# A hybrid attention and mixture-of-experts layer on one core: when plain sums leave PSUM, which slots the router's tiles take, and where a count is read

## The chip, the cores and the metric

The kernel runs on 1 core of a Trainium2 chip. The metric is the device time of one execution in microseconds, as the median of a few runs. One more execution was profiled; all rows below are from that one. Its engines are PE (TensorE: matmuls; PEld is its weight load), DVE (VectorE), ACT (ScalarE), POOL (GpSimd) and SP (SyncE, which here only issues transfers and loads registers). PE, DVE and ACT share PSUM, the small memory into which matmuls add their sums.

## The reference

One decoder layer on 1024 tokens of width 1024. Everything is float32.

```python
h = rms_norm(x, norm1_g) * (1 + scale1) + shift1
aq, ak, av, bq, bk, bv = split(h @ w_in)
x = x + gate1 * (concat(dilated_attention(aq, ak, av), diff_attention(bq, bk, bv)) @ w_out)
h2 = rms_norm(x, norm2_g) * (1 + scale2) + shift2
logits = h2 @ w_router + b_router                  # 32 experts
top_val, top_idx = top_k(logits, 4); gates = softmax(top_val)
# every token goes to its 4 experts:
gu = xe @ w_gate_up[e] + b_gate_up[e]              # 1024 -> 2048
g = minimum(gu[:, :1024], 7); u = clip(gu[:, 1024:], -7, 7)
y = ((u + 1) * g * sigmoid(1.702 * g)) @ w_down[e] + b_down[e]
out = x + gate2 * sum over the token's experts of gate * y
```

## The kernel before

**Stages.** The kernel first makes projections and attention (to about 585 us). Then the router stage (to about 745 us) does the output projection block by block (8 blocks of 128 tokens), the second norm, the logits, the top 4 and each token's place in its experts' lists. The rest is 32 experts, one after another, fully unrolled, and a loop for tokens that did not fit an expert's planned capacity.

**Order.** From the attention stage on, the instructions of PE, ACT, DVE and SP stand in the order in which the Python code issues them (`manual_schedule`). POOL's order is chosen by a scheduler, which may bring an instruction forward as far as its data and its tile allow.

**Router (class `Block`).** For block b, `logits` makes the top 4, `places` (two blocks later) counts positions and fills `pay` (token number and gate, 4 pairs per token), `counted` makes `sli` (4 list places per token), and `scattered` has POOL write the 4 columns of `pay` into the table `tab` in device memory at the places in `sli` (L982, 4 indirect transfers per block). The token number in `pay` comes from a POOL iota (L944). A tile that comes from pool `sm` has 3 buffers (`sm3`, bufs=3), so block b takes the memory of block b-3 and its first writer waits until the last reader of that memory is done. A tile that comes from pool `rt` lives to the end. Only the last block takes `pay` and `sli` from `rt`. The same POOL queue also computes the reciprocal roots for the norms (L111), which DVE finishes (L115 to L117); then DVE makes `pay`, `hot` and `tg`, and PE multiplies these in `listed` (L960).

**An expert (function `expert`).** C is the expert's planned number of tokens (96 to 200; over 128 it is two blocks). Weights arrive in chunks of 1 MB, 12 per expert: 10 "split" chunks go through ACT (`hb`, high part, L826) and DVE (`ha`, low part, L813) into two halves each, through a ring of 6 chunk buffers; 2 "plain" chunks of `w_down` are used by PE as they are. `products` multiplies the split ones (L1196, L1202). After gate and up products come the plain chunks: `pg` is one PSUM tile with two banks; 4 sums (`place(0)` to `place(3)`), two per bank, over two halves `kh` of the inner dimension (L1252, 4 matmuls per sum and half in the code, two instructions each). In the second half ACT moves the sums out to `yl` with scale and bias (L1263): after `j == 1` sums 0 and 1, after `j == 3` sums 2 and 3. Then `between(kh)` transposes the next expert's tokens (L1174, and on ACT, DVE and POOL `xx`, `xb`), and `products(C, s_a, t0 + 16)` makes the other half of the output columns; `back` transposes (L1285), scales (`y`, L1286) and has POOL add the rows into the output (L1182). `banks()` takes one of 4 PSUM tiles in rotation. `done()` is a point at which transfers of later chunks are issued and later chunks are split, to targets fixed in a table: one half chunk is split at the `done()` after `j == 1` of the second half, one at the end of the half.

**Overflow.** `overflow()` (third expert) computes `tot`, the number of extra blocks. `nc.values_load(tot...)` (L1371) puts it into a register of each of the five engines, and `tc.For_i(0, n_over, 1)` (L1372) runs that many times.

Of the kernel before, what the change touches and what calls it, by code (L numbers as in the profile page):

```python
# [9 lines left out]
F32 = mybir.dt.float32  # L10
# [66 lines left out]
def hybrid_layer(ctx: ExitStack, tc: tile.TileContext, x, c_t, w_ada, b_ada_t, b_ada, norm1_t, w_in,  # L77
# [107 lines left out]
    with ExitStack() as st:  # L185
# [332 lines left out]
        with ExitStack() as so:  # L518
# [334 lines left out]
            class Block:  # L853
# [84 lines left out]
                def places(self):  # L938
                    pp = ps3.tile([P, 512], F32, name="po")
                    nc.tensor.matmul(pp[:, :E], upper, self.msk, start=True, stop=False)  # L940
                    nc.tensor.matmul(pp[:, :E], ones, mcum, start=False, stop=True)
                    nc.vector.reciprocal(self.den, self.den)
                    pay = (sm if self.b < NB - 1 else rt).tile([P, TOPK, 2], F32, name="pay")
                    nc.gpsimd.iota(pay.bitcast(I32)[:, :, 0], pattern=[[0, TOPK]], base=self.b * P, channel_multiplier=1)  # L944
                    nc.vector.tensor_scalar_mul(pay[:, :, 1], self.ge, self.den)

                    hot = sm.tile([P, len(BLOCKS0) * P], F32, name="hot", bufs=2)
                    nc.vector.tensor_scalar(hot, srow, pp[:, 0:1], self.msk[:, 0:1], op0=OP.is_equal, op1=OP.mult)
                    tg = sm.tile([P, 3], F32, name="tg")
                    nc.gpsimd.iota(tg[:, 0:1], pattern=[[0, 1]], base=self.b * P - S, channel_multiplier=1,  # L950
                                   allow_small_or_imprecise_dtypes=True)
                    nc.gpsimd.memset(tg[:, 2:3], 1.0)
                    g0 = sm.tile([P, TOPK], F32, name="g0")
                    nc.vector.tensor_mul(g0, self.sel[:, :, 0], pay[:, :, 1])
                    nc.vector.tensor_reduce(tg[:, 1:2], g0, axis=AX.X, op=OP.add)
                    self.hot, self.tg, self.pay, self.pp = hot, tg, pay, pp
# [13 lines left out]
                def counted(self):  # L970
                    pos = sm.tile([P, E], F32, name="pos")
                    nc.vector.tensor_add(pos, self.pp[:, :E], ebase)
                    nc.vector.tensor_mul(self.sel, self.sel, pos[:, None, :].to_broadcast([P, TOPK, E]))
                    slf = sm.tile([P, TOPK], F32, name="slf")
                    nc.vector.tensor_reduce(slf, self.sel, axis=AX.X, op=OP.add)
                    self.sli = (sm if self.b < NB - 1 else rt).tile([P, TOPK], I32, name="sli")
                    nc.vector.tensor_copy(self.sli, slf)
                    nc.vector.tensor_add(mcum, mcum, self.msk)

# [112 lines left out]
    with ExitStack() as se:  # L1092
# [30 lines left out]
        def done(high=0, low=0):  # L1123

            spent[0] += high
            spent[1] += low
            i, q = divmod(event[0], len(TG))
            event[0] += 1
            pump(i * NSP + TG[q])
            for t in todo:  # L1130
                t[0] -= 1
            while todo and todo[0][0] <= 0:
                todo.pop(0)[1]()
# [72 lines left out]
        def expert(i, st, between):  # L1206
            C, bc = st["C"], st["bc"]
            a = ap_.tile([P, KT, C], F32, name="ay")
            s_a = operand(C, "ax", "ab")
            t0, d0 = i * NSP, i * NCH + PLAIN[0]  # L1210

            def joined(dst, p, f, more):

                t = ap_.tile([P, 2, C], F32, name="tb", bufs=2)
                for j in range(2):
                    nc.scalar.activation(t[:, j], p[:, j, C:2 * C], AF.Identity, bias=bc[:, f + j:f + j + 1], scale=1.0)  # L1216
                if more:
                    nc.vector.scalar_tensor_tensor(dst, t, more, p[:, :, :C], op0=OP.add, op1=OP.add)
                else:
                    nc.vector.tensor_add(dst, p[:, :, :C], t)  # L1220

            for half in range(2):
                pg = products(C, st["x"], t0 + 8 * half)
                gt = ap_.tile([P, 4, C], F32, name="gt")
                for q in range(2):
                    joined(gt[:, 2 * q:2 * q + 2], pg[q], 4 * half + 2 * q, 0.0)
                sg = ap_.tile([P, 4, C], F32, name="su")
                nc.scalar.activation(sg, gt, AF.Sigmoid, scale=1.702)
                nc.vector.tensor_mul(gt, gt, sg)
                done(high=2, low=4)  # L1230
                pg = products(C, st["x"], t0 + 8 * half + 4)
                ut_ = ap_.tile([P, 4, C], F32, name="su")
                for q in range(2):
                    ut = ut_[:, 2 * q:2 * q + 2]
                    f = 4 * half + 2 * q
                    joined(ut, pg[q], KT + f, 1.0)
                    nc.vector.tensor_scalar(ut, ut, 8.0, -6.0, op0=OP.min, op1=OP.max)
                    nc.vector.scalar_tensor_tensor(a[:, f:f + 2], gt[:, 2 * q:2 * q + 2], GATE7, ut, op0=OP.min, op1=OP.mult)
                done(high=2, low=4)


            pg = banks()

            def place(j):
                return pg[:, j // 2, j % 2 * 256:j % 2 * 256 + C]

            ah, ab, _ = s_a
            for kh in range(2):
                raw = raws.pop(d0 + kh)
                for j in range(4):  # L1250
                    for k in range(4):
                        nc.tensor.matmul(place(j), raw[:, k, j * P:(j + 1) * P], a[:, 4 * kh + k],  # L1252
                                         start=(kh + k + j % 2 == 0), stop=(kh == 1 and k == 3 and j % 2 == 1))
                    if j == 1:
                        f = slice(4 * kh, 4 * kh + 4)
                        nc.scalar.activation(ah[:, f, :C], a[:, f], AF.Copy)  # L1256
                        nc.vector.tensor_sub(ah[:, f, C:], a[:, f], ah[:, f, :C].bitcast(F32))
                        nc.gpsimd.tensor_copy(ab[:, f], ah[:, f, :C].bitcast(F32))  # L1258
                    if kh and j % 2:
                        if j == 1:  # L1260
                            yl = ap_.tile([P, 4, C], F32, name="yl")
                        for f in (j - 1, j):
                            nc.scalar.activation(yl[:, f], place(f), AF.Identity,  # L1263
                                                 bias=bc[:, 2 * KT + f:2 * KT + f + 1], scale=g2c[:, f:f + 1])
                    if j == 1:
                        done()
                freed["p"] += 1
                done()
                between(kh)
            pg = products(C, s_a, t0 + 16)  # L1270
            yh = ap_.tile([P, KT, C], F32, name="ay")
            ys = [yl[:, f] for f in range(4)] + [yh[:, f] for f in range(4)]
            for j in range(4):
                f, p = 4 + j, pg[j // 2][:, j % 2]
                t = ap_.tile([P, 2, C], F32, name="tb", bufs=2)[:, 0]
                nc.scalar.activation(t, p[:, C:2 * C], AF.Identity, bias=bc[:, 2 * KT + f:2 * KT + f + 1], scale=g2c[:, f:f + 1])  # L1276
                nc.vector.scalar_tensor_tensor(ys[f], p[:, :C], g2c[:, f:f + 1], t, op0=OP.mult, op1=OP.add)  # L1277
            done(high=2, low=4)

            def back():  # L1280
                for (r0, n), sl in zip(st["blocks"], st["slots"]):
                    y = ap_.tile([P, D], F32, name="y", bufs=2)
                    py = banks().rearrange("p g (k c) -> p (g k) c", k=4)
                    for k in range(KT):
                        nc.tensor.transpose(py[:n, k], ys[k][:, r0:r0 + n], ident)  # L1285
                    nc.scalar.activation(y[:n].rearrange("p (k c) -> p k c", k=KT), py[:n], AF.Copy, scale=sl[:n, 1:2])  # L1286
                    scatter(y, sl, n)
            later(1, back)
# [66 lines left out]
        for i in range(E):  # L1355
            if i == 2:
                tot = overflow()
            nxt = stage_g(i + 1) if i + 1 < E else None
            expert(i, st, lambda g: nxt and stage_t(nxt, g))
            st = nxt  # L1360
# [4 lines left out]
    with ExitStack() as sf:  # L1365
# [2 lines left out]
        ps5 = sf.enter_context(tc.tile_pool(name="ps5", bufs=2, space=PSUM))  # L1368
        gate2 = fp.tile([P, D], F32, name="gate2")
        nc.sync.dma_start(gate2, bcast_rows(modd, 3 * D, D))  # L1370
        n_over = nc.values_load(tot[0:1, 0:1], min_val=0, max_val=P)  # L1371
        with tc.For_i(0, n_over, 1) as i:  # L1372
            ov = fp.tile([1, 2], I32, name="ov")
            nc.sync.dma_start(ov, ovd[ds(i, 1), :])
# [96 lines left out]
```

## Time and profile before

| | |
|---|---|
| median of 3 runs | 2157.39 us (2155.97 to 2163.31) |
| the profiled execution, device time | 2155.82 us |
| its span in the trace | 2154.0 us |
| mean granted PE clock over the span | 0.985 |
| PE matmul busy, share of the span | 95% |
| weight traffic and all else, mean | 255 GB/s over the span |

The span is the part of the device time that the trace covers; 1.8 us lie around it. A row's busy time of PE counts matmuls that overlap each other. An idle time in a row is put down to the event that ended it.

### The profile page before, as it was taken

Reading aid. Unit: us, or ns where it says so; the run is one execution under the profiler, and the core shown is the slowest. Engines: PE = TensorE matmul, PEld = TensorE weight load, DVE = VectorE, ACT = ScalarE, POOL = GpSimd, SP = SyncE. Lnnn points to the kernel's source line nnn. Section 1 sums busy time; section 2 is a strip of 40 time slices with the busy share of each in tenths; the row PEclk is TensorE's granted clock in tenths of the full one; section 3 lists DMA queues with packets and bytes.
Section 4 is the critical chain, followed back from the end, with each engine's and each line's share of the span. In section 5 each row is a group of like instructions: output and inputs, shape, how many; then the busy total and the mean of one; then the engine's idle time right before and its main releaser. Section 6 shows DMA issues by size and latency. Waiting matters only on the chain.

```text
span 2154.0 us, 43837 instructions
## 1 busy us (share of the span) xinstructions
PE 2046.7 (95%) x16922; PEld 1914.8 (89%) x16922; DVE 1631.7 (76%) x2838; ACT 1357.8 (63%) x2391; POOL 481.7 (22%) x466
## 2 busy tenths in 40 slices
PE   6999999999999699999999999999999999999997
PEld 6877778998887599999998999999999999999996
DVE  6587765776666778788787877878878878878884
ACT  3522314777643367677677677777877777768774
POOL 2245532111013411112111222112111211211211
PEclk9999999999999799999999999999999999999998
DMA  8267886442233498899799999989999999999993
GB/s 296 67 161 220 217 237 164 112 114 70 90 129 145 158 338 293 268 337 343 268 295 347 289 315 317 324 296 349 309 321 300 355 319 330 325 332 322 332 321 81
DMA packets 273655, 549.53 MB, mean 255 GB/s; under 512 B 31796, under 2 KB 31812, under 8 KB 273316
## 3 DMA queue, kind: packets, MB, share of 16 engines
q1 hardware_dynamic: 251507, 490.61, 67.4%
q0 software_dynamic: 21936, 56.09, 11.2%
q8 instruction: 134, 2.20, 0.4%
q14 instruction: 78, 0.63, 0.1%
HBM read 501.84 MB, written 44.78 MB: 254 GB/s over the span
## 4 chain that ended last, share of the span: by engine, by line
PE 61%; ACT 5%; DMA 3%; DVE 3%; issue 2%; POOL 1%; POOLq 0%; SPq 0%; ACTq 0%; DVEq 0%
PE gu L1196 30%; PE gu L1202 13%; PE gu L1252 10%; PE gu L1285 2%; ACT hb L826 2%; PE gu L1174 2%; PE po L605 1%; ACT yl L1263 1%; DMA eraw<-in_w_down_dram 1%; DMA eraw<-in_w_gate_up_dram 1%; PE pss L567 1%; DMA tab<-pay,sli 1%; PE pt L598 1%; POOL tab L982 1%; DVE ha L813 0%
## 5 line engine op out<-in xcount | busy, mean ns | idle before, releaser
L813 DVE TENSOR_TENSOR ha<-eraw,hb 128x1024 bf16<-128x1024 f32 x640 | 760.0, 1240 | 7.7 <-ACT hb L826 7.7
L826 ACT ACTIVATE hb<-eraw 128x1024 fp32r<-128x1024 f32 x640 | 634.1, 1050 | 21.2 <-DMA eraw<-in_w_down_dram 15.3
L1196 PE MATMUL gu<-xx,hb 128*128 128x256 f32 (+13 forms) x4096 | 586.3, 299 | 2.2 <-DVE xx L1178 2.2
L1196 PEld LDWEIGHTS gu<-xx,hb 128*128 128x128 f32 x4096 | 552.9, 189 | 2.6 <-DVE xx L1178 2.4
L1202 PEld LDWEIGHTS <-ha 128*128 128x128 bf16 x5120 | 310.6, 97 | 11.8 <-issue 1.5
L1252 PE MATMUL gu<-ay,draw 128*128 128x128 f32 (+19 forms) x2048 | 277.9, 292 | 36.4 <-ACT yl L1263 32.9
L1252 PEld LDWEIGHTS gu<-ay,draw 128*128 128x128 f32 x2048 | 260.5, 192 | 44.5 <-ACT yl L1263 39.7
L1202 PE MATMUL gu<-xb,ha 128*128 128x128 bf16 (+19 forms) x4096 | 271.6, 224 | 0.0
L1216 ACT ACTIVATE tb<-gu,bcol 128x128 f32<-128x128 f32 (+19 forms) x512 | 156.9, 369 | 89.8 <-PE gu L1202 80.8
L1182 POOL DMA_INDIRECT out_dram<-y,slot x47 | 79.7, 1695 | 404.9 <-ACT y L1286 263.0
L1146 POOL DMA_INDIRECT xg<-h2d,slot x47 | 65.9, 1401 | 393.0 <-PE gu L1174 86.8
L1196 PE MATMUL gu<-ax,hb 128*128 128x256 f32 (+13 forms) x1024 | 144.5, 298 | 0.0
L1276 ACT ACTIVATE tb<-gu,bcol,g2c 128x128 f32<-128x128 f32 (+19 forms) x128 | 56.3, 465 | 132.4 <-PE gu L1202 104.8
L1196 PEld LDWEIGHTS gu<-ax,hb 128*128 128x128 f32 x1024 | 137.4, 188 | 0.6
L571 DVE CUSTOM_DVE_ANT_0 p<-pss,bias 128x1024 f32<-128x1024 f32 (+7 forms) x128 | 94.4, 755 | 52.1 <-ACT p L580 23.5
L1277 DVE SCALAR_TENSOR_TENSOR ay<-gu,g2c,tb 128x128 f32<-128x128 f32 (+19 forms) x128 | 46.2, 362 | 113.9 <-ACT tb L1276 113.9
L1258 POOL CAST ab<-ax 128x512 bf16<-128x512 f32 (+19 forms) x64 | 69.7, 1094 | 263.7 <-ACT ax L1256 263.7
L605 PE MATMUL po<-vsb,pT 128*128 128x64 f32 (+1 forms) x864 | 111.3, 275 | 2.9 <-ACT pT L599 1.4
L605 PEld LDWEIGHTS po<-vsb,pT 128*128 128x128 f32 x864 | 105.4, 194 | 5.8 <-ACT pT L599 2.0
L580 ACT ACTIVATE p<-p,mn 128x1024 f32<-128x1024 f32 (+7 forms) x128 | 98.6, 773 | 11.9 <-DVE mn L571 11.2
L111 POOL TENSOR_TENSOR rrs<-vrs,nhalf 128x8 f32<-128x8 f32 (+2 forms) x48 | 66.1, 1377 | 169.6 <-DVE vrs L109 167.8
L459 PE MATMUL pp<-wh,hb 128*128 128x512 f32 x240 | 100.5, 419 | 0.0
(275 smaller groups left out, 3080.6 us busy)
## 6 DMA issues: line engine op xcount, KB each, us to landing
eraw<-in_w_gate_up_dram SPq DMA_DIRECT2D x256, 1024.0 KB
draw<-in_w_down_dram SPq DMA_DIRECT2D x64, 1024.0 KB
eraw<-in_w_down_dram SPq DMA_DIRECT2D x64, 1024.0 KB
wraw<-in_w_ada_dram SPq DMA_DIRECT2D x32, 512.0 KB
wraw<-in_w_in_dram SPq DMA_DIRECT2D x23, 512.0 KB
hb<-in_w_ada_dram SPq DMA_DIRECT2D x16, 512.0 KB
qd<-tt POOLq DMA_DIRECT2D x32, 256.0 KB, 3.7
kd<-tt POOLq DMA_DIRECT2D x32, 256.0 KB, 4.0
```

Source lines behind the costliest of these rows:

```text
L459: nc.tensor.matmul(pp, hh[b][:, k], wh[:, kk], start=(k == 0), stop=False)
L571: nc.vector.tensor_tensor_reduce(p[:, :n], pss[:, :n], bias[:, (NB - 1 - ib) * P:(NB - 1 - ib) * P + n], -1.0, 3.0e38, OP.add, OP.min, mn)
L580: nc.scalar.activation(p, p, AF.Exp, bias=self.mn[c], scale=-1.0, accum_out=self.l[:, c:c + 1])
L605: nc.tensor.matmul(self.po[:, :w], self.pT[:, k], vsb[self.br][:, k, self.h * w:(self.h + 1) * w], start=(k == 0), stop=(k == self.ib))
L813: nc.vector.tensor_tensor(parts[t][1], raws[c][:, 2 * q:2 * q + 2], parts[t][0].bitcast(F32), OP.subtract)
L826: nc.scalar.activation(h_, raws[c][:, 2 * q:2 * q + 2], AF.Copy)
L1182: nc.gpsimd.indirect_dma_start(out=out, out_offset=bass.IndirectOffsetOnAxis(ap=sl.bitcast(I32)[:n, 0:1], axis=0), in_=y[:n], in_offset=No ...
L1196: nc.tensor.matmul(pg[j // 2][:, j % 2, :max(256, 2 * C)], w[k][0][:, j * P:(j + 1) * P], xk[k], start=(k == 0), stop=False)
L1202: nc.tensor.matmul(pg[j // 2][:, j % 2, C:2 * C], w[k][1][:, j * P:(j + 1) * P], xb[:, k], start=False, stop=(k == KT - 1))
L1216: nc.scalar.activation(t[:, j], p[:, j, C:2 * C], AF.Identity, bias=bc[:, f + j:f + j + 1], scale=1.0)
L1252: nc.tensor.matmul(place(j), raw[:, k, j * P:(j + 1) * P], a[:, 4 * kh + k], start=(kh + k + j % 2 == 0), stop=(kh == 1 and k == 3 and j % ...
L1258: nc.gpsimd.tensor_copy(ab[:, f], ah[:, f, :C].bitcast(F32))
```

## The change

Three edits. In the router, `pay` and `sli` come from `rt` with one buffer per block, for every block. In the expert, the four sums of the plain half go to `yl` together, after `j == 3` of the second half, where before two of them went after `j == 1`; the `done()` after `j == 1` stays where it was, and so now stands ahead of all four. The register loads of `tot` move from ahead of the overflow loop to the start of the sixth expert (`i == 5`).

```diff
--- before.py
+++ after.py
@@ -940,7 +940,7 @@
                     nc.tensor.matmul(pp[:, :E], upper, self.msk, start=True, stop=False)
                     nc.tensor.matmul(pp[:, :E], ones, mcum, start=False, stop=True)
                     nc.vector.reciprocal(self.den, self.den)
-                    pay = (sm if self.b < NB - 1 else rt).tile([P, TOPK, 2], F32, name="pay")
+                    pay = rt.tile([P, TOPK, 2], F32, name="pay", bufs=NB)
                     nc.gpsimd.iota(pay.bitcast(I32)[:, :, 0], pattern=[[0, TOPK]], base=self.b * P, channel_multiplier=1)
                     nc.vector.tensor_scalar_mul(pay[:, :, 1], self.ge, self.den)
 
@@ -973,7 +973,7 @@
                     nc.vector.tensor_mul(self.sel, self.sel, pos[:, None, :].to_broadcast([P, TOPK, E]))
                     slf = sm.tile([P, TOPK], F32, name="slf")
                     nc.vector.tensor_reduce(slf, self.sel, axis=AX.X, op=OP.add)
-                    self.sli = (sm if self.b < NB - 1 else rt).tile([P, TOPK], I32, name="sli")
+                    self.sli = rt.tile([P, TOPK], I32, name="sli", bufs=NB)
                     nc.vector.tensor_copy(self.sli, slf)
                     nc.vector.tensor_add(mcum, mcum, self.msk)
 
@@ -1256,14 +1256,12 @@
                         nc.scalar.activation(ah[:, f, :C], a[:, f], AF.Copy)
                         nc.vector.tensor_sub(ah[:, f, C:], a[:, f], ah[:, f, :C].bitcast(F32))
                         nc.gpsimd.tensor_copy(ab[:, f], ah[:, f, :C].bitcast(F32))
-                    if kh and j % 2:
-                        if j == 1:
-                            yl = ap_.tile([P, 4, C], F32, name="yl")
-                        for f in (j - 1, j):
-                            nc.scalar.activation(yl[:, f], place(f), AF.Identity,
-                                                 bias=bc[:, 2 * KT + f:2 * KT + f + 1], scale=g2c[:, f:f + 1])
-                    if j == 1:
                         done()
+                if kh:
+                    yl = ap_.tile([P, 4, C], F32, name="yl")
+                    for f in range(4):
+                        nc.scalar.activation(yl[:, f], place(f), AF.Identity,
+                                             bias=bc[:, 2 * KT + f:2 * KT + f + 1], scale=g2c[:, f:f + 1])
                 freed["p"] += 1
                 done()
                 between(kh)
@@ -1355,6 +1353,8 @@
         for i in range(E):
             if i == 2:
                 tot = overflow()
+            if i == 5:
+                n_over = nc.values_load(tot[0:1, 0:1], min_val=0, max_val=P)
             nxt = stage_g(i + 1) if i + 1 < E else None
             expert(i, st, lambda g: nxt and stage_t(nxt, g))
             st = nxt
@@ -1368,7 +1368,6 @@
         ps5 = sf.enter_context(tc.tile_pool(name="ps5", bufs=2, space=PSUM))
         gate2 = fp.tile([P, D], F32, name="gate2")
         nc.sync.dma_start(gate2, bcast_rows(modd, 3 * D, D))
-        n_over = nc.values_load(tot[0:1, 0:1], min_val=0, max_val=P)
         with tc.For_i(0, n_over, 1) as i:
             ov = fp.tile([1, 2], I32, name="ov")
             nc.sync.dma_start(ov, ovd[ds(i, 1), :])
```

## Rows read from the trace of the kernel before

**Rows 1.** The page's first section: busy us (share of the span) and instructions.
```profile
PE 2046.7 (95%) x16922; PEld 1914.8 (89%) x16922; DVE 1631.7 (76%) x2838; ACT 1357.8 (63%) x2391; POOL 481.7 (22%) x466
```

**Rows 2.** Waits, 780 to 2154 us: waiter, releaser, total us, times, longest.
```profile
PE gu L1252 <- ACT yl L1263: 32.9, 32, 3.2
PE gu L1252 <- DVE ay L1238: 2.5, 2, 2.1
```

**Rows 3.** Timeline of one expert, 918 to 942 us: start, us, engine, line.
```profile
921.68 3.79 PE L1252 MATMUL gu<-ay,draw 128*128 128x128 f32 x32
...
925.31 0.94 PE L1174 MATMUL gu<-ident,xg 128*128 128x128 f32 x8
...
926.18 2.05 PE L1252 MATMUL gu<-ay,draw 128*128 128x128 f32 x16
...
928.27 0.81 ACT L1263 ACTIVATE yl<-gu,bcol,g2c 128x128 f32<-128x128 f32 x2 [0.33 <-PE gu L1252]
928.97 1.05 ACT L826 ACTIVATE hb<-eraw 128x1024 fp32r<-128x1024 f32 x1
929.13 2.05 PE L1252 MATMUL gu<-ay,draw 128*128 128x128 f32 x16 [0.90 <-ACT yl L1263]
...
931.01 0.94 PE L1174 MATMUL gu<-ident,xg 128*128 128x128 f32 x8
931.22 0.81 ACT L1263 ACTIVATE yl<-gu,bcol,g2c 128x128 f32<-128x128 f32 x2 [1.20 <-PE gu L1252]
...
931.88 4.06 PE L1196 MATMUL gu<-ax,hb 128*128 128x256 f32 x32
...
934.28 1.34 DVE L1178 TENSOR_TENSOR xx<-gu,xx 128x1024 fp32r<-128x1024 f32 x2
...
937.56 2.25 PE L1196 MATMUL gu<-xx,hb 128*128 128x272 f32 x16
```

**Rows 4.** Windows: stretch, us, busy PE, PEld, DVE, ACT, POOL, PEclk, DMA share, GB/s.
```profile
1339.00:2070.00 731.00, 714.57 (x7047) 700.13 (x7046) 603.72 (x801) 551.79 (x882) 141.71 (x128) 1.00 0.98 325
1468.00:1511.00 43.00, 42.08 (x409) 41.48 (x409) 35.79 (x48) 32.49 (x52) 7.93 (x8) 1.00 1.03 353
```

**Rows 5.** Waits of ACT's splits for weights, 780 to 2154 us; columns of Rows 2.
```profile
ACT hb L826 <- DMA eraw<-in_w_down_dram: 14.4, 9, 7.6
ACT hb L826 <- DMA eraw<-in_w_gate_up_dram: 5.8, 3, 2.9
```

**Rows 6.** Waits in the router, 629.7 to 702.6 us.
```profile
POOL pay L944 <- DMA tab<-pay,sli: 10.5, 4, 3.2
DVE qr L115 <- POOL rr L111: 6.2, 4, 2.1
...
PE p L960 <- DVE tg L955: 5.0, 4, 2.3
```

**Rows 7.** Windows of the router where the granted clock is low; columns of Rows 4.
```profile
661.00:664.00 3.00, 3.00 (x9) 2.31 (x9) 1.11 (x5) 1.76 (x5) 0.00 (x0) 0.50 0.43 175
694.90:701.70 6.80, 6.80 (x27) 6.11 (x27) 4.73 (x12) 2.48 (x7) 0.17 (x2) 0.50 0.19 77
```

**Rows 8.** Timeline of POOL, 0 to 30 us.
```profile
3.61 0.20 POOL L944 IOTA pay<- 128x4 int32 x1
21.14 1.01 POOL L111 TENSOR_TENSOR rrs<-vrs,nhalf 128x1 f32<-128x1 f32 x1 [17.33 <-DVE vrs L109]
```

**Rows 9.** Instructions of L1371: duration ns min/median/max, first and last start.
```profile
L1371 SPq TENSOR_LOAD <-tot x1: 757/757/757, 850.0 to 850.0; - x1
L1371 PEldq TENSOR_LOAD <-tot x1: 484/484/484, 2140.6 to 2140.6; - x1
...
L1371 POOLq TENSOR_LOAD <-tot x1: 502/502/502, 2142.1 to 2142.1; - x1
```

**Rows 10.** Timeline of the end, 2139 to 2144 us.
```profile
2142.38 1.46 POOL L1182 DMA_INDIRECT out_dram<-y,slot  x1 [12.81 <-ACTq L1372]
```

**Rows 11.** Waits of SP, 2128 to 2155 us.
```profile
SPq L1372 <- DMA out_dram<-y,slot: 4.5, 1, 4.5
```

## Prediction

> **What bounds the kernel now.** I read the page first, then the waits of PE, then a timeline of one expert. PE is busy 95% of the span [rows 1], so time is won only where PE waits, runs at a lower clock, or restarts. In the expert stage PE's waits have one cause that repeats: 32 times, once in each expert, it waits for ACT's `yl`, 32.9 us in all [rows 2]. The timeline shows where: the first half of the plain sums runs 32 matmul instructions without a stop, the second half runs 16, stands still while ACT moves the first two sums out, and runs 16 more [rows 3]. Next I read what feeds PE. The transfers are nearly full: between 1339 and 2070 us they move 325 GB/s at a busy share of 0.98, and the fullest stretch reaches 353 GB/s [rows 4]; ACT's splits already wait 20.2 us (14.4 + 5.8, 12 times) for weights that are late [rows 5]. Last come the waits of the router [rows 6] and the windows in which PE's granted clock is low there [rows 7].
>
> **Experts: the sums leave together.** With all four evacuations behind the last product nothing of L1263 stands between PE's matmuls. What that gives is read from one expert: the first half takes 925.31 - 921.68 = 3.63 us up to the next PE work, the second 931.01 - 926.18 = 4.83 us [rows 3]. The difference, 1.20 us, is the 0.90 us of waiting and the 0.3 us that PE loses when its matmuls run out and start again. 32 x 1.20 = 38.4 us. Of the 32.9 us of waiting, 32 x 0.90 = 28.8 us are regular; the other 4.1 us belong to a few experts in which ACT came late [rows 2]. Those go too, unless ACT's lateness meets PE elsewhere; between 0 and 4.1 I take 2 us.
>
> What it adds: ACT's evacuations end later. Four take about 2 x 0.81 = 1.62 us after the last sum instead of 0.81. Two things stand behind them. First, a PSUM tile: four rotate, and where the next expert has two blocks (16 of 32 experts) the transposes take two, so the second tile of the following products is the one that `yl` is read from. In the expert shown the last sum ends at 931.18, so the four would end at 932.84; PE starts those products at 931.88 and is at their second tile after 8 of 32 matmuls, 4.06 / 4 = 1.0 us later, at 932.9 [rows 3]. It just fits. From nothing to 0.12 us in 16 experts is 0 to 2 us; I take 1. Second, the next tokens' `xx`: DVE ends it at 935.62 and PE needs it at 937.56 [rows 3]; 0.81 of these 1.94 us are used up, so this costs nothing. Without that cover it would be up to 0.81 us per expert. The split of 1.05 us that now stands ahead of the four runs while PE multiplies, where ACT was waiting for PE before.
>
> The clock has no term here: in the long stretch of experts the granted clock is 1.00, waits and all [rows 4]. By the Trainium skill ("TensorE: Matmul & The Clock Gate", "A second HAM failure mode") short idle times between groups of matmuls can make the clock swing; by it 32 waits would each have a slow piece behind them, and if each were the 3.0 us at half speed of the router [rows 7], another 32 x 1.5 = 48 us would come back. The trace does not agree, and I leave it out.
>
> **What the faster experts ask of the transfers.** 38.4 us of a stage of 1374 us (780 to 2154) is 2.8%: 325 GB/s become 334, under the 353 that a full stretch moved [rows 4]. So it fits on average, not everywhere. A late chunk becomes later by what PE gained since the queue last had room. If that is one or two experts (1.2 to 2.4 us) at each of the 12 places, ACT waits 14 to 29 us more. So far PE pays a third of ACT's waits: the 4.1 us above and 2.5 us for `ay` [rows 2] of 20.2 us. A third of 14 to 29 is 5 to 10; the ends are 0 and 29. I take 6 us.
>
> **Router: own slots.** Four times POOL's iota for `pay` waits for the scatters into `tab` to land, 10.5 us in all. Behind it on POOL stand the roots of the norms (L111); DVE waits for those 6.2 us, and PE then waits 5.0 us for `tg` [rows 6]. With a slot per block no iota takes memory that a scatter still reads. Like the one that lies in `rt` now, the iotas can run at the start, where POOL has 17.33 us of idle time and 8 x 0.20 us find room [rows 8]; without that cover they cost 1.6 us. DVE's 6.2 us cover PE's 5.0 us, so the 5.0 goes, less perhaps 0.5. After two of these waits PE's granted clock is 0.50, its 1.2 GHz level, for 3.0 and 6.8 us [rows 7]; 9.8 us at half speed is 4.9 us lost. If the waits go the clock may stay up. From 0 to 4.9 I take 3.5. Together 8 us, between 3 and 10. The handover to the first expert stays as long and starts earlier.
>
> **The count's registers.** The load of 0.50 us on POOL at the end [rows 9] runs while POOL's last scatter starts (2142.1 and 2142.38 [rows 10]), and SP then waits 4.5 us for that scatter to land [rows 11]. So taking it away gives 0 to 0.5 us; I take 0. In the sixth expert PE's load takes 0.48 us [rows 9], between nothing (matmuls already handed out cover it) and 0.5; ACT, DVE and POOL behave alike, and SP (0.76 us) has waits of its own. I take 0.4.
>
> **Sum**, against the profiled execution's 2155.82 us: -38.4 - 2 + 1 + 6 - 8 + 0.4 = -41.0, so 2114.8, and 2115 us is my prediction. The median of the runs is 1.6 us above that execution, inside the range.
>
> **Rivals.**
> - Transfers are the bound. For: busy share 0.98 and 20.2 us of ACT waits [rows 4, 5]. Against: 353 GB/s in a full stretch. Then the 29 us all fall on PE in place of 6: 2138 us. Chance 0.17.
> - The router's wait moves. PE finds the next thing late (ACT or DVE), or the clock falls all the same; the router gives nothing: 2123 us. For: POOL, DVE and PE form one chain there. Against: DVE's saving is larger than PE's wait [rows 6]. Chance 0.10.
> - The wait stays. Sums 0 and 1 lie in another bank than the one PE writes next, so what holds PE may be no read of theirs. Then only the router counts: 2155.8 - 8 + 0.4 = 2148 us. Against: PE goes on 0.05 us after the second `yl` ends (929.08, 929.13 [rows 3]), and 32 of 32 waits name it [rows 2]. By the Trainium skill ("PSUM — Partial Sum Buffer", "Summary: rules for kernel authors") one reads PSUM during matmuls from a different bank and evacuates promptly; by that rule the early evacuation would cost nothing, and the change would only hold the tile longer. The trace disagrees with the first part. Chance 0.05.
> - Slower than before: ACT comes late to all four, because the split ahead of them waits for weights, and in the 16 experts with a two-block successor PE stops at the tile. It decides from 41 / 16 = 2.6 us each; at 3.2 us each, the longest wait so far [rows 2], 51 us go and it ends at 2166. Against: 12 late chunks in all [rows 5]. Chance 0.04.
>
> **Numbers.** The forecast itself (2105 to 2124) has 0.64. Its lower end takes all 4.1, 10 and no loss to transfers: 2155.8 - 38.4 - 4.1 - 10 = 2103. The range reaches up into the first two rivals: 2105 to 2130. About 0.3% (6.5 us) is what a measurement of this kernel can tell from no change. Faster by more than that: forecast, the first two rivals and about half of the third, 0.93; within: 0.03; slower: 0.04.
>
> **What would show it.** After: no wait of PE L1252 for `yl`; both halves of the plain sums 3.6 us long where C is 128; no wait of `pay` for `tab`, and eight iotas at the start; granted clock 1.00 in the router up to the handover; ACT's waits for weights at 30 to 50 us. It is wrong if a wait of about 1 us stands before the second tile of the following products, if ACT's waits for weights reach PE in most experts, or if L960 waits as before.

## The result, and the profile after

The kernel after takes 2110.61 us (median of 4 runs, 2109.98 to 2113.01), the kernel before, now with 4 runs, 2158.26 us. The ratio is 0.9778, 95% interval 0.9759 to 0.9797. The forecast was 2115 us, range 2105 to 2130. The profiled execution after takes 2109.98 us, 45.84 us less than the one before. I cut both traces at three points that each has (first gate matmul of the router, L878; first expert product, L1196; end of the last matmul) and compared the pieces:

| stretch, us | before | after | change | predicted |
|---|---|---|---|---|
| up to the router | 586.13 | 584.28 | -1.85 | 0 |
| router | 159.83 | 152.79 | -7.04 | -8 |
| 32 experts | 1394.99 | 1358.20 | -36.79 | -33.0 |
| tail | 13.09 | 12.93 | -0.16 | 0 |

The first line is spread between executions: nothing there was changed, and over the first six runs below this stretch differs from the one before by +0.3 to -2.2 us, whichever edits the kernel has.

The page's first section, after (answers to [rows 1]):

```profile
PE 2035.8 (97%) x16922; PEld 1910.2 (91%) x16922; DVE 1635.9 (78%) x2838; ACT 1355.8 (64%) x2391; POOL 493.8 (23%) x466
```

PE has as many instructions as before and is busy for a larger share of a shorter span. Waits of PE after, from the first expert's products on, 741 to 2108 us (answers to [rows 2]); the first two rows of the answer:

```profile
PE gu L1252 <- DVE ay L1238: 4.4, 4, 1.9
PE gu L1283 <- DVE ay L1275: 0.5, 1, 0.5
```

The row of 32.9 us for `yl` is gone; what stands at the top now was the second row before. Timeline of the same place in the same expert, 905 to 925 us (answers to [rows 3]):

```profile
909.27 3.79 PE L1252 MATMUL gu<-ay,draw 128*128 128x128 f32 x32
...
912.90 0.94 PE L1174 MATMUL gu<-ident,xg 128*128 128x128 f32 x8
...
913.77 3.84 PE L1252 MATMUL gu<-ay,draw 128*128 128x128 f32 x32
...
917.45 0.94 PE L1174 MATMUL gu<-ident,xg 128*128 128x128 f32 x8
917.65 1.51 ACT L1263 ACTIVATE yl<-gu,bcol,g2c 128x128 f32<-128x128 f32 x4 [1.15 <-PE gu L1252]
...
918.32 4.06 PE L1196 MATMUL gu<-ax,hb 128*128 128x256 f32 x32
...
921.90 1.34 DVE L1178 TENSOR_TENSOR xx<-gu,xx 128x1024 fp32r<-128x1024 f32 x2
...
923.99 1.25 PE L1196 MATMUL gu<-xx,hb 128*128 128x272 f32 x8
```

Both halves are now one row of 32 matmuls, 3.63 us (909.27 to 912.90) and 3.68 us (913.77 to 917.45) up to the next work of PE. The four evacuations end at 917.65 + 1.51 = 919.16; the following products begin at 918.32 and are at their second tile 1.0 us later, at 919.3, and their row is 4.06 us long, as before. DVE ends `xx` at 923.24, and PE takes it at 923.99: the cover has shrunk from 1.94 to 0.75 us, and it still holds.

A window of the expert stage (answers to [rows 4]; same columns):

```profile
1300.00:2030.00 730.00, 728.86 (x7196) 716.88 (x7195) 621.66 (x822) 563.52 (x904) 153.09 (x134) 1.00 0.99 335
```

ACT's waits for weights, 740 to 2108 us (answers to [rows 5]):

```profile
ACT hb L826 <- DMA eraw<-in_w_down_dram: 28.0, 14, 6.9
ACT hb L826 <- DMA eraw<-in_w_gate_up_dram: 6.7, 3, 3.4
```

The transfers give 335 GB/s, as worked out (334), and the splits wait 34.7 us; in the whole expert stage before, counted from 740 us as here, it was 21.1 us. PE is busy 728.86 of 730 us all the same.

The mean clock of 1.00 over such a window hides short pieces at the lower level. Before, one lies in the expert stage, just ahead of the window of [rows 4] and behind the longest of the 32 stops. PE's timeline there, and a window:

```profile
1326.50 3.72 PE L1252 MATMUL gu<-ay,draw 128*128 128x140 f32 x16 [3.17 <-ACT yl L1263]
```

```profile
1326.30:1329.70 3.40, 3.20 (x14) 3.20 (x15) 3.40 (x5) 1.09 (x2) 2.60 (x1) 0.50 1.04 392
```

After, there are two, in the second halves of the ninth and the thirteenth expert, each behind a stop for `ay`:

```profile
1126.37 5.90 PE L1252 MATMUL gu<-ay,draw 128*128 128x140 f32 x32 [1.90 <-DVE ay L1238]
...
1299.56 0.74 PE L1252 MATMUL gu<-ay,draw 128*128 128x140 f32 x4 [1.87 <-DVE ay L1238]
```

```profile
1126.50:1129.90 3.40, 3.40 (x14) 3.14 (x15) 3.33 (x6) 3.40 (x5) 0.20 (x1) 0.50 0.85 313
1300.50:1303.90 3.40, 3.15 (x13) 3.15 (x14) 3.40 (x5) 3.26 (x5) 0.00 (x0) 0.51 1.00 350
```

Each such piece of 3.4 us at half speed costs some 1.7 us: the 32 matmuls at 1126.37 take 5.90 us, and the 32 of the same expert's first half take 4.03.

In the router the eight iotas now stand together at the start. POOL's timeline, 0 to 30 us (answers to [rows 8]):

```profile
3.62 0.74 POOL L944 IOTA pay<- 128x4 int32 x8
21.30 1.01 POOL L111 TENSOR_TENSOR rrs<-vrs,nhalf 128x1 f32<-128x1 f32 x1 [16.94 <-DVE vrs L109]
```

POOL's waits in the router no longer name `tab` for `pay`, and this is PE's only wait in 629 to 703 us (answers to the last of [rows 6]):

```profile
PE p L960 <- DVE tg L955: 0.2, 1, 0.2
```

The clock did not stay up throughout. Windows of the router (answers to [rows 7]):

```profile
655.30:658.30 3.00, 3.00 (x11) 2.37 (x10) 1.13 (x4) 1.76 (x5) 0.00 (x0) 0.52 0.42 175
658.30:662.00 3.70, 3.70 (x17) 3.02 (x16) 3.39 (x14) 0.72 (x2) 1.04 (x1) 0.93 0.60 210
662.00:679.00 17.00, 17.00 (x95) 14.41 (x95) 11.23 (x37) 6.80 (x24) 6.66 (x9) 1.00 0.50 187
679.00:697.00 18.00, 17.95 (x102) 14.73 (x100) 11.83 (x37) 7.21 (x25) 7.42 (x10) 1.00 0.44 161
```

PE's timeline ahead of the first of them:

```profile
652.86 0.58 PE L960 MATMUL p<-tg,hot 128*128 128x3 f32 x4 [0.16 <-DVE tg L955]
653.29 1.95 PE L918 MATMUL po<-wr,hT 128*128 128x32 f32 x16
655.08 0.48 PE L878 MATMUL pm<-hb,oh 128*128 128x512 f32 x1
655.39 0.60 PE L879 MATMUL pm<-hb,ol 128*128 128x512 f32 x1
```

One low piece of some 3 us is left (0.52, close to the lower level of 1.2 GHz), where before there were two, of 3.0 and 6.8 us. Ahead of it PE waited 0.16 us only, and ran 20 matmuls of 3 and 32 columns. The same 20 run in the next two blocks at 1.00. In the trace of the run that evacuates after the third product (below) PE has the same wait here (0.15 us), and its clock is not low in the router before 714 us. So neither the wait nor the narrow matmuls alone tell when the clock falls.

Past 703 us there is a wait that the kernel before did not have. The place matmul of the seventh block, before and after:

```profile
717.01 0.30 PE L940 MATMUL po<-msk,upper 128*128 128x32 f32 x2
```

```profile
708.07 0.41 PE L940 MATMUL po<-msk,upper 128*128 128x32 f32 x2 [1.79 <-DVE nm L933]
```

Counted from the start of the router, PE comes here 8.9 us earlier than before, and then waits 1.79 us for DVE.

The loads of the count, two rows of the line's instructions (answers to [rows 9]):

```profile
L1357 PEldq TENSOR_LOAD <-tot x1: 485/485/485, 962.1 to 962.1; - x1
...
L1357 POOLq TENSOR_LOAD <-tot x1: 505/505/505, 2096.5 to 2096.5; - x1
```

The end in the timeline (answers to [rows 10]):

```profile
2096.70 1.46 POOL L1182 DMA_INDIRECT out_dram<-y,slot  x1 [11.72 <-ACTq L1371]
```

SP's wait there, 2085 to 2109 us (answers to [rows 11]):

```profile
SPq L1371 <- DMA out_dram<-y,slot: 4.3, 1, 4.3
```

PE's load moved to the sixth expert; POOL's, whose order the scheduler makes, stayed at the end.

### The profile page after: what moved, and what is told of

Its sections match the earlier page's. It is cut to its first block, busy times and chain, and to the rows that moved or that the text cites. A ratio compares the mean times of both kernels' runs of the same rounds, so it can differ in the third digit from the quotient of the medians.

```text
span 2108.2 us, 43814 instructions
## 1 busy us (share of the span) xinstructions
PE 2035.8 (97%) x16922; PEld 1910.2 (91%) x16922; DVE 1635.9 (78%) x2838; ACT 1355.8 (64%) x2391; POOL 493.8 (23%) x466
## 4 chain that ended last, share of the span: by engine, by line
PE 62%; DVE 4%; DMA 4%; ACT 2%; issue 2%; POOL 0%; POOLq 0%; SPq 0%; ACTq 0%; DVEq 0%
PE gu L1196 30%; PE gu L1202 13%; PE gu L1252 11%; DMA eraw<-in_w_down_dram 2%; PE gu L1283 2%; PE gu L1174 2%; PE po L605 1%; DMA eraw<-in_w_gate_up_dram 1%; DVE ha L813 1%; PE pss L567 1%; PE pt L598 1%; PE pm L880 0%; PE pm L878 0%; PE pm L879 0%; ACT hb L826 0%
## 5 line engine op out<-in xcount | busy, mean ns | idle before, releaser
L1196 PE MATMUL gu<-xx,hb 128*128 128x256 f32 (+13 forms) x4096 | 586.6, 299 | 2.5 <-DVE xx L1178 2.5
L1196 PEld LDWEIGHTS gu<-xx,hb 128*128 128x128 f32 x4096 | 553.3, 189 | 3.1 <-DVE xx L1178 2.8
L1252 PE MATMUL gu<-ay,draw 128*128 128x128 f32 (+19 forms) x2048 | 271.5, 291 | 4.4 <-DVE ay L1238 4.4
L1182 POOL DMA_INDIRECT out_dram<-y,slot x47 | 78.3, 1667 | 390.6 <-ACT y L1284 225.9
L1146 POOL DMA_INDIRECT xg<-h2d,slot x47 | 71.7, 1525 | 339.7 <-DVE ay L1238 89.6
L1196 PE MATMUL gu<-ax,hb 128*128 128x256 f32 (+13 forms) x1024 | 145.0, 299 | 0.2 <-DVE ax L1257 0.2
L1196 PEld LDWEIGHTS gu<-ax,hb 128*128 128x128 f32 x1024 | 137.5, 188 | 1.3 <-DVE ax L1257 0.5
L1220 DVE TENSOR_TENSOR gt<-gu,tb 128x256 f32<-128x256 f32 (+19 forms) x128 | 55.4, 445 | 60.8 <-ACT tb L1216 53.1
```

The lines of the kernel that those rows point to most:

```text
L1146: nc.gpsimd.indirect_dma_start(out=xg[:n], out_offset=None, in_=h2d, in_offset=bass.IndirectOffsetOnAxis(ap=sl.bitcast(I32)[:n, 0:1], axis=0))
L1182: nc.gpsimd.indirect_dma_start(out=out, out_offset=bass.IndirectOffsetOnAxis(ap=sl.bitcast(I32)[:n, 0:1], axis=0), in_=y[:n], in_offset=No ...
L1196: nc.tensor.matmul(pg[j // 2][:, j % 2, :max(256, 2 * C)], w[k][0][:, j * P:(j + 1) * P], xk[k], start=(k == 0), stop=False)
```

## The experiments

Theory: PE waited for `yl` because the evacuation reads the tile that the next product writes, though in another bank; without that wait the experts are worth some 37 us and the router's slots 7 us, and the late weights take little back. Theories of the wait, as the expectations name them: the order between evacuation and product is kept for a whole PSUM tile, or it has to do with the bank or with the moment. Other rivals: the transfers are now the bound; `sli`'s slots count too; the count's loads cost time. Three groups of kernels ran, each beside the kernel before on the same chip (2152.02, 2153.72 and 2155.27 us); the ratios are to that.

**One edit at a time.** Each kernel is the one before with one of the three parts of the diff.

The sums only:

> The kernel before with only the expert's edit: all four sums go to yl after the last one. My theory: this edit carries nearly all of the gain. The expert stage was 1395.0 us before and 1358.2 us with all edits, so it should be about 37 us shorter here, the two halves of the plain sums equally long, and the time 36 to 39 us below before; the router's waits for the landing of tab (10.5 us) stay. Rival, that the edits need each other (a router that ends earlier gives the transfers a lead on which the experts then draw): the expert stage gains clearly less than 37 us, 25 to 32.

2119.72 us, ratio 0.9844 (0.983 to 0.9858). Experts 1359.06 us, router 159.75, as before; PE still waits for `tg` there (3.8 us in 630 to 703 us).

The slots only:

> The kernel before with only the router's edit: pay and sli with a slot per block. My theory: 7 us less, all of it between the start of the router (586.1 us before) and the first product of the first expert (746.0), and an expert stage as long as before (1395). The 1.85 us that the kernel with all edits gained ahead of the router are chance: then they need not be here. Rival: POOL standing at the first pay until the attention stage frees its memory (37 us of waiting) cost those 1.85 us; then they are here too, and the total is 9 us.

2148.74 us, ratio 0.9975 (0.9963 to 0.9987). Router 152.55 us (-7.28), experts 1396.46 us; the waits for `yl` stay (31.8 us, 32 times). So each edit acts in its own stage. By their ratios the two kernels gain 33.6 and 5.3 us, less than the 36 to 39 and the 7 expected. The stages shorten by 35.9 and 7.3 us, but that is against the one trace of before, whose execution took 2155.82 us; before has a median of 2152.02 us in this group. So a difference of two stages can be off by a few us.

The count only:

> The kernel before with only the register loads of the count moved into the sixth expert. My theory: nothing that can be measured, from -0.5 to +0.5 us; the stretch from PE's last product to the end stays at 13.1 us. Rival: the loads at the end cost what they last, and 0.5 us or more go there; or PE stands for its 0.48 us in the sixth expert and the time rises by that.

2156.27 us, ratio 1.0015 (1.0004 to 1.0025). I had not expected a loss. At the sixth expert nothing is to be seen: measured from the first expert product, the plain sums start 0.4 us later than before in each of the first six experts alike, and 0.3 in the next two. Steps come later: -1.0 us at the ninth expert, +1.5 at the tenth, +1.8 at the fourteenth. The two traced executions differ by 0.4 us in all (2156.19 and 2155.82), so these traces do not hold the loss that the medians show.

**All edits, and all but the count.**

> The kernel with all three edits again, beside kernels with fewer. The single edits measured -33.6 us (sums), -5.3 us (slots) and +3.2 us (count): -35.7 us together, while all edits at once had measured -47.8 us (ratio 0.9778) beside another set of runs of before. My theory: the edits add up, and the difference is that of one set of runs to the next; then this one measures a ratio between 0.979 and 0.983 (36 to 45 us). Rival: the edits need each other; then the ratio is again 0.978 or lower.

> All edits but the count's: the register loads stand ahead of the overflow loop as before. My theory: the same as all edits within 2 us, since the register loads run beside other work at either place. Rival: the 3.2 us by which the count's edit alone came out slower are real; then this kernel is about 3 us faster than all edits.

2113.15 us, ratio 0.9807 (0.9793 to 0.982), and 2110.79 us, 0.9799 (0.9785 to 0.9812). The intervals overlap. The two part by 1.8 us at the thirteenth expert and are 1.0 us apart at the stage's end, so again nothing happens where the loads stand. The count's edit gives nothing; whether it costs 1 to 3 us, by shifting when weights land or otherwise, was not settled.

**Bank or tile: evacuating after the third product.** All edits, but sums 0 and 1, in the first bank of the tile, leave after product 2 and not after product 3:

```diff
-                if kh:
-                    yl = ap_.tile([P, 4, C], F32, name="yl")
-                    for f in range(4):
...
+                    if kh and j > 1:
+                        if j == 2:
+                            yl = ap_.tile([P, 4, C], F32, name="yl")
+                        for f in ((0, 1) if j == 2 else (2, 3)):
```

> The kernel with all edits, except that sums 0 and 1 go to yl after the third sum (j == 2) and sums 2 and 3 after the fourth. Sums 0 and 1 are in the tile's first bank, the third and fourth in its second. Theory A: what held PE is that any read of the tile by ACT is put in order with every later write to the tile, whichever bank. Then PE now stands ahead of the fourth sum, in every expert, for about 0.9 us (ACT reads the first two only when the third is done), and the time is back near before: 2140 to 2160. Theory B: only accesses to one bank are put in order. Then the fourth sum waits for nothing and the time is that of all edits, 2110. Theory C: PE was held at the first write to the second bank only, by something else than yl: no wait ahead of the fourth sum, 2110, and a wait ahead of the third as before would come back.

2147.92 us, ratio 0.9974 (0.9964 to 0.9985). The gain in the experts is gone. PE's waits, 741 to 2150 us, first row:

```profile
PE gu L1252 <- ACT yl L1264: 32.3, 32, 3.4
```

The same expert in its timeline:

```profile
917.13 2.94 PE L1252 MATMUL gu<-ay,draw 128*128 128x128 f32 x24
...
920.11 0.81 ACT L1264 ACTIVATE yl<-gu,bcol,g2c 128x128 f32<-128x128 f32 x2 [0.26 <-PE gu L1252]
...
920.97 1.16 PE L1252 MATMUL gu<-ay,draw 128*128 128x128 f32 x8 [0.90 <-ACT yl L1264]
```

Now 24 matmuls run, PE stands still for the same 0.90 us, and 8 follow. ACT reads one bank, product 3 goes to the other, which product 2 has already written; the only thing the two share is the tile. The trace names what holds PE: the weight load at 920.97 waits for a semaphore that ACT's second evacuation raises. Before, the first weight load of product 2 waits for it (929.12). The order is thus one that the program's instructions keep.

**The reverse: two tiles.** The kernel before, early evacuation and all, with sums 0 and 1 in one PSUM tile and 2 and 3 in another:

```diff
-            pg = banks()
+            pgs = [banks() for _ in range(2)]
...
-                return pg[:, j // 2, j % 2 * 256:j % 2 * 256 + C]
+                return pgs[j // 2][:, 0, j % 2 * 256:j % 2 * 256 + C]
```

> The kernel before with one edit: the four plain sums of a half stand in two PSUM tiles of two banks each in place of one tile of four; the first two are still evacuated behind product 1 and the last two at the end. Theory (the order is kept per tile): product 2 writes another tile than the evacuation reads, so TensorE no longer waits for yl (32.3 us in the run that held the sums in one tile), and the kernel gains about 34 us (ratio about 0.984, as with the sums' edit alone). Rival: the wait has to do with the evacuation's time and not with the tile; then it stays at some 32 us and the ratio is near 1.00. Second rival: the finer tiles come free later and a new wait at the first product of a half appears, with a ratio in between.

(The expectation miscounts: a tile has two banks. Before, one tile held the four sums; here two tiles do, each in its first bank, for both halves of an expert.)

2125.94 us, ratio 0.9858 (0.9843 to 0.9873). The same expert in its timeline:

```profile
923.01 3.84 PE L1252 MATMUL gu<-ay,draw 128*128 128x128 f32 x32
925.10 0.81 ACT L1263 ACTIVATE yl<-gu,bcol,g2c 128x128 f32<-128x128 f32 x2 [0.33 <-PE gu L1252]
```

The wait for `yl` is gone without moving any evacuation, and none of these 32 waits for the evacuations' semaphore, so it was the tile. The 32 matmuls take 3.84 us, as in the kernel after, though ACT reads two sums meanwhile. PE's waits, 755 to 2125 us, first two rows:

```profile
PE gu L1196 <- DVE xx L1178: 4.2, 11, 0.7
PE gu L1174 <- DVE su L1218: 3.9, 3, 1.6
```

Both are new, and they are the price: each expert now draws one tile more from the four that rotate, so PE comes sooner upon a tile that DVE still reads. PE's idle time in the expert stage is 12.95 us, against 5.91 in the kernel after and 37.33 before (all gaps between matmuls over 0.05 us). The stage takes 1365.90 us, 6.8 more than with the sums' edit alone.

The same with the router's slots, as a candidate for something faster than all edits:

> The kernel before with the sums in two PSUM tiles and with the router's slots per block; nothing else. Theory: both gains add, 2109 to 2113 us (ratio 0.980), equal to all edits. It would be faster than all edits, by 1 us or more, only if the earlier evacuation of the first two sums also shortens something at the end of a half. Rival: the tiles' rotation costs a wait per half (0.1 to 0.5 us, 62 halves), 2116 to 2140 us.

2116.44 us, ratio 0.982 (0.9807 to 0.9834): not faster. Its stage of experts (1362.40 us) is 4.0 us longer than that of sums and slots (1358.44).

**Are the transfers the bound?** All edits, but the 49 indirect transfers that add the experts' rows into the output (L1182; the expectation's 47, and 2 of the first expert) are left out, so the experts' part is missing from the output:

```diff
-            nc.gpsimd.indirect_dma_start(
...
-                in_=y[:n], in_offset=None, compute_op=OP.add)
+            if True:
+                return
```

> All edits, but the experts' rows are not added into the output: the 47 indirect transfers of L1182 are left out, the other work stays. It asks how much late weights still cost. My theory: after the edits PE pays only the 4 waits for ay (4.4 us) for late weights; without the rows' traffic ACT's waits for weights fall from 34.7 us to under 10, the expert stage shortens by 4 to 8 us, and another 4 to 6 us go at the end, where nothing waits for the last rows to land: about 2098. Rival, that the transfers are now the bound of the stage: its rate is set by bytes, and it shortens by 25 us or more, to below 2080.

2097.23 us, ratio 0.9734 (0.9716 to 0.9752). About half of what that is below the kernel after is the tail (5.67 us instead of 12.93), which no longer waits for the last of them. ACT's waits for weights, 740 to 2110 us:

```profile
ACT hb L826 <- DMA eraw<-in_w_down_dram: 13.8, 8, 3.7
```

The window of the expert stage:

```profile
1300.00:2030.00 730.00, 729.26 (x7227) 717.85 (x7226) 621.24 (x824) 562.01 (x904) 110.49 (x107) 1.00 0.94 322
```

ACT waits 13.8 us in place of 34.7 (not under 10, as expected), and the experts take 1352.0 us in place of 1358.2. So 20.9 us less of waiting on ACT is worth 6.2 us at most on PE; the transfers take a little, and do not set the time. PE's waits for `ay` fall from 4.4 to 0.6 us, and no piece at the lower clock is left in the expert stage, where after has two (some 3.4 us). New waits for `ax` take 1.3 us back (1.5 in place of 0.2). That makes 5.9 of the 6.2 us.

**The split behind the evacuations.** All edits, with the split that stands ahead of the four evacuations put behind them:

```diff
-                        done()
+                        if not kh:
+                            done()
...
+                    done()
```

> All edits, with the done() that follows the second sum of the second half moved behind the four evacuations, so that no split stands ahead of them on ACT. The slower rival of the prediction said that a split which waits for weights could hold up all four and, through the PSUM tile, PE. The profile after shows no wait of PE for yl. My theory: no difference within 2 us, or slightly slower, since the split comes later and its chunk's buffer is free later. Rival: 3 us or more faster.

2110.80 us, ratio 0.9798 (0.9785 to 0.9812): no difference from all edits. Being behind a split costs nothing that this run can tell.

**Which slots.** All edits, but `sli` keeps its two buffers:

```diff
-                    self.sli = rt.tile([P, TOPK], I32, name="sli", bufs=NB)
+                    self.sli = (sm if self.b < NB - 1 else rt).tile([P, TOPK], I32, name="sli")
```

> All edits, but sli keeps its one pair of buffers for all blocks; only pay has a slot per block. Theory: the wait at POOL's iota for pay carried the whole of the router's loss, so the router (first gate matmul to first expert product) takes about 152.8 us as with all edits, and the kernel 2111 to 2113 us. Rival: sli's slots matter too; then the router is 2 to 7 us longer and the kernel 2113 to 2120 us.

2108.49 us, ratio 0.9783 (0.9769 to 0.9796), router 152.91 us: `pay` alone carries it.

**The low clock that is left.** All edits, with `TA = 5` for `TA = 4`, so that more products of the next block stand ahead of the router's place matmul:

> All edits, with three more product steps of the next block issued ahead of the router's place matmul. Theory: the wait of 1.8 us ahead of the place matmul in the block with low clock goes, and the kernel gains up to 2 us (2109 to 2112 us). Rival: the wait moves to the later chain of the block and the time is the same or up to 3 us longer.

2111.42 us, ratio 0.9794 (0.978 to 0.9807). One window of the router in the kernel with `pay` alone:

```profile
655.00:662.00 7.00, 7.00 (x30) 5.79 (x30) 4.87 (x17) 2.48 (x7) 0.65 (x1) 0.76 0.45 142
```

The same in the kernel with `TA = 5`:

```profile
655.00:662.00 7.00, 7.00 (x36) 5.78 (x36) 4.79 (x19) 2.49 (x7) 1.04 (x1) 1.00 0.67 235
```

The low piece is gone, 36 matmuls run where 30 did. Yet the router takes 152.23 us, 0.6 less than after, and other kernels with own slots for `pay` read 152.1 to 152.9 us, with a low piece here or without. From 679 to 697 us PE is now busy 17.25 us of 18, and not 17.95, with new waits for `ol` and `oh` (0.7 and 0.5 us over the router). The wait for `nm` stays (4.5 us, 5.0 after). The 1.8 us of it that the theory puts into the block with the low clock stand in a later one, at 708.07 us after, and are 1.3 us here.

## Why the prediction was right, step by step

- **The bound.** PE was the bound, and it gained where it stopped. Over 31 experts the second plain half was longer than the first by 43.1 us in all; now by 5.1. With the last expert (its two halves run without other work between them, 8.43 to 7.35 us) the plain sums gave 39.1 us, against 40.4 for the steps of 38.4 and 2. The regular part was 36.5 of 37.2 us over 31 experts. The part of ACT's lateness was 1.5 of 2. Before, three late second halves were together 6.1 us longer than the rest; after, three are 4.6 us longer. The late stops for `yl` went, but PE's waits for `ay` rose from 2.5 to 4.4 us, and behind two of them the second half runs at the lower clock for 3.4 us.
- **The PSUM tile** was put at 1 us and cost none that a wait shows: the row of products is 4.06 us long before and after, and no wait for `yl` stands in the list. The cover of `xx` held too (0.3 us, once, in the expert stage).
- **Late weights** is the step whose size was off. It stood at +6 us. Outside the plain sums the stage lost 39.1 - 36.8 = 2.3 us, and that holds the tile and the registers as well; 2.0 of it is the stop for `ay` ahead of the second half in the thirteenth expert. ACT's extra waiting was 13.6 us (34.7 less 21.1), just under the low end of the 14 to 29, and outside the plain sums PE paid no more than those 2.3 us of it, a sixth and not a third. Counted whole, as the late second halves and the long stops for `ay` ahead of them, lateness cost PE 8.2 us before (6.1 and 2.1) and 8.4 after (4.6 and 3.8): 13.6 us more of waiting on ACT cost PE almost nothing more. This term, the tile's and the registers' were to take back 7.4 us; that 5.1 of them stayed away, less the 1.3 that the plain sums fell short, is the 3.8 us by which the experts did better, and most of the 4.8 by which the whole did. The stretch ahead of the router gave 1.85 more, without a cause in the change.
- **Router.** 7.04 us of the 8. The waits behind the iota went (5.0 to 0.2 us on PE in the four blocks of [rows 6]). By the windows the clock lost 4.9 us before and loses 1.7 now, so it gave back 3.2 of the 3.5: the piece of 6.8 us is gone, one of 3 us is there, after next to no wait. What the prediction had no term for is the new wait of 1.79 us for `nm` in the seventh block. The three make 6.2 of the 7.04 us. What the remaining piece is worth was not shown: the 0.6 us of the run with `TA = 5` is within the spread of the router's time between kernels.
- **Registers.** 0.4 was taken and no cost is seen in the sixth expert; nothing came back at the end either, where SP waits for the last rows as before (4.3 us, 4.5 before).
- **The rival that the wait stays** was beaten by this change and explained by two runs. By the Trainium skill ("PSUM — Partial Sum Buffer", "Summary: rules for kernel authors") PSUM that is read while a matmul runs should be in a different bank. The sums are in different banks in every kernel here. With a tile for each pair the trace agrees (no wait, 32 matmuls in 3.84 us while ACT reads). The 32.3 us of waits with both banks in one tile do not speak against the rule, as the prediction took the waits of before to do: they are a semaphore wait that the program itself has, and it follows the tile.
- **The other rivals.** Transfers as the bound: ruled out by the run without the rows out. The router's wait moving came in part: 1.79 us at `nm`, and one low piece. ACT late to all four: the split ahead or behind made no difference, and PE's waits name no tile.
- **The clock** in the experts: the prediction read 1.00, "waits and all", from a window that starts just behind the one low piece of before. Of the 32 stops for `yl` only the longest, 3.17 us, has a low piece behind it. So the regular stops of 0.90 us give no support to the rule on short idle times ("TensorE: Matmul & The Clock Gate" of the Trainium skill, "A second HAM failure mode"), and leaving out its 48 us was right. But with one low piece before and two after, the clock took back some 1.7 us that the sum does not have.
- **Luck.** The total is within 5 us because misses cancel in part: the stretch ahead of the router and the late weights came out better than forecast, the plain sums (with the low clock in them) and the router worse.

Open: why the count's edit alone measured 0.15% slower; and after which stops the clock falls (before, a stop of 2.09 us for `ay` at 1145.75 left it at 1.00; after, it fell behind those of 1.90 and 1.87 us).

## What to carry to other kernels

Look for a wait that returns once per unit of work, measure it against a twin of the same work that has none (here the first half against the second), and multiply; that gave the plain sums' gain to 3%. When a matmul waits for an evacuation, ask which tile they share before asking which bank, and weigh the two cures: evacuating later lengthens a tile's life, splitting it uses up rotation. A transfer queue at a share of 0.98 is a reason to look, not a bound: what counts is how much of the feeding engine's waiting reaches the engine that sets the end.

## What the runs showed that I had not expected

- PE stopped for an evacuation of another bank of the same tile, 0.90 us at a time where ACT was not late, once in each of 32 experts, in both places of the half where it was put. A semaphore wait in the program makes this stop.
- PE's granted clock fell to 0.52 after a wait of only 0.16 us, behind 20 matmuls of 3 and 32 columns; in the experts the stops of 0.90 us left it at 1.00, and it was 0.50 for 3.4 us behind one stop of 3.17 us before and two of 1.90 and 1.87 us after.
- The transfers' busy share reads 0.99 at 335 GB/s, and 0.94 at 322 GB/s without the rows out: leaving out 49 indirect transfers took away 20.9 us of ACT's waiting for weights.
- Register loads of 0.46 to 0.55 us each on PE, ACT, DVE and SP in the middle of the expert stage cost no visible time on PE.
